# A score product over 128 rows instead of 64, its other half zeros, and narrower bias tiles

## The chip, the core and the metric

The kernel runs on one core of a Trainium2 chip. The metric is the device time of one execution in microseconds, the median of several runs. TensorE multiplies matrices into PSUM; VectorE, ScalarE and GpSimd work element by element, and a queue on SyncE issues the transfers between DRAM and SBUF.

## What is computed

One layer of a hybrid decoder trunk on an input of 2048 tokens by 1024 features: a normalization, one input projection, three parallel branches (differential attention, a gated short convolution, an RWKV-7 recurrence), an output projection, a residual and a last normalization. The change touches attention alone. Each of its 4 heads has two maps of width 64, whose causal softmaxes are subtracted:

```python
qf = (q.astype(jnp.float32) * scale).reshape(b, nb, Q_BLOCK, h, 2, ATT_QK_DIM).swapaxes(0, 1)
...
bias = jnp.transpose(table[t5_causal_bucket(dist)], (2, 0, 1))
logits = jnp.einsum('bqhmd,bkhmd->bhmqk', qb, kf) + bias[None, :, None]
logits = jnp.where(dist >= 0, logits, NEG_INF)
p = jax.nn.softmax(logits, axis=-1)
a = p[:, :, 0] - lam * p[:, :, 1]
return jnp.einsum('bhqk,bkhd->bqhd', a, vf)
```

## The kernel before

All large products are made in a rounded 32-bit format. To keep precision, an operand is split into a high part (the rounded value) and a low part (what is left), and a product is the sum of high by high, high by low and low by high. The work is in two halves of 1024 tokens. In each half an RWKV stage is followed by an attention stage; between their products TensorE gets products of a filler stream (the input projection on line 343, in the second half the output projection on line 1194), a number of them after each step that the stages' code states. TensorE's order is that in which the code is written; the other engines' and the DMA queue's order is set by a scheduler when the program is built.

In `attention`, `load_k` brings 512 columns of K for a head into `rawk`, each map's 64 rows twice, one copy over rows 0 to 63 and one over 64 to 127. GpSimd rounds it into `K` (line 861) and, for each map, replaces the copy in the other map's rows by the low part (line 864). So 128 rows of `K[:, m]` hold high and low part of map m. `load_q` does likewise for 256 queries: `QH` (line 889) holds the high part of a map's queries in both copies, so that one product over 128 rows is high by high plus high by low. `QL` (line 893) holds the low part, 64 rows for each map. `load_v` splits V in the same way.

`scores` goes through the blocks of up to 512 keys of a tile of 128 queries. For each map it makes a pair of products into a score buffer `S` of PSUM (there are three): line 937 with `QH` over 128 rows, line 938 with `QL` over 64 rows, with the queries as the stationary operand and K as the moving one. Then VectorE adds the bias where the block lies near the diagonal (line 942, from the tile `bt` of the head), takes the maximum (line 943), and ScalarE the exponential (line 946), which frees the buffer. `combine` scales and subtracts the two maps (VectorE on line 986); `values` transposes the result (line 1021), splits it (ScalarE on line 1027, VectorE on line 1028) and multiplies with V (lines 1012 to 1014). `att_setup` prepares the bias tiles once, early, by way of DRAM (line 840).

Of the kernel before, what the change touches and what calls it, by code (L numbers as in the profile page):

```python
# [30 lines left out]
GW = 32 // NG  # L31
# [114 lines left out]
def trunk(ctx, tc, a, o, phases="RTO"):  # L146
# [62 lines left out]
    def dtile(name, shape):  # L209
        return dr.tile(list(shape), F32, name=name)  # L210

    # row blocks of the gated mix, transposed: heads by 256 tokens, conv and rwkv by 512
    mixd = [[dtile(f"mx{k}_{i}", (P, 256 if k < 4 else 512)) for i in range(8 if k < 4 else 4)] for k in range(8)]
    pT = {}

# [6 lines left out]
    hh = [[None] * NK, [None] * NK]  # L222
    hl = [[None] * NK, [None] * NK]

    # ------------------------------------------------------------------ normalized input
    def stats(c):
        """1/rms of the tokens of a chunk of the second half, one column per 128 tokens."""
        t0 = HT + c * CK
        ss = cp.tile([P, 2, 4], F32, name=f"ss1{c}")
        for j in range(4):  # L230
            for i in range(2):
                xt = e2("xt")
                dma(xt, a["x"][t0 + j * P:t0 + (j + 1) * P, i * CK:(i + 1) * CK])
                act(xt, xt, AF.Square, accum_out=ss[:, i, j:j + 1])
        tt(ss[:, 0], ss[:, 0], ss[:, 1], ALU.add)
        ts(ss[:, 0], ss[:, 0], 1.0 / D, NORM_EPS, ALU.mult, ALU.add)
        rs = cp.tile([P, 4], F32, name=f"rs1{c}")
        nc.gpsimd.tensor_tensor(rs, ss[:, 0], mexp[:, :4], ALU.pow)
        return rs
# [24 lines left out]
    rscale = [None, None]  # L264

    def stats0(c, xs, pool, raw):
        """1/rms of the tokens, broadcast; with raw, the products with the unscaled input come first."""
        acc = [pool.tile([P, CK], F32, name="acc0", bufs=2) for _ in range(2)]
        for k in range(NK):
            if raw:  # L270
                hh[c][k] = pool.tile([P, CK], F32R, name=f"xh{k}")
                hl[c][k] = pool.tile([P, CK], F32R, name=f"xl{k}")
                act(hh[c][k], xs[k], AF.Copy, scale=V("norm_g", k))
                stt(hl[c][k], xs[k], V("norm_g", k), hh[c][k].bitcast(F32), ALU.mult, ALU.subtract)
            add = nc.gpsimd.tensor_tensor if k % 2 else tt
            if k < 2:
                act(acc[k], xs[k], AF.Square)
            else:
                sq = pool.tile([P, CK], F32, name="sq0", bufs=3)
                act(sq, xs[k], AF.Square)  # L280
                add(acc[k % 2], acc[k % 2], sq, ALU.add)

        def finish():
            sp = pw("ss0")
            for j in range(4):
                for i in range(2):
                    mm(sp[:, j:j + 1], acc[i][:, j * P:(j + 1) * P], C("ones"), start=(i == 0), stop=(i == 1))
            ss = cp.tile([P, 4], F32, name=f"ss0{c}")
            ts(ss, sp[:, 0:4], 1.0 / D, NORM_EPS, ALU.mult, ALU.add)
            rs = cp.tile([P, 4], F32, name=f"rs0{c}")  # L290
            nc.gpsimd.tensor_tensor(rs, ss, mexp[:, :4], ALU.pow)
            return rs

        return finish
# [10 lines left out]
            dma(xk, a["xT"][k * P:(k + 1) * P, t0:t0 + CK])  # L305
            scale_h(c, k, xk, bc, nc.gpsimd.tensor_tensor if k % 2 else tt)

    # ------------------------------------------------------------------ input projection
    wpool = [None]

    early_w = {}
# [92 lines left out]
        yield from inproj(T_RW + i, ev, chunks)  # L404

    def both(*steps):
        """The products of the steps, for the first chunk of all of them before the second."""
        for c in range(2):
            for f, args in steps:
                yield from f(*args, (c,))  # L410
            yield ("chunk", c)
# [39 lines left out]
        return [(inproj, (T_CC + ct, ev_cc)), (inproj, (T_CH + ct, ev_ch)), (inproj, (T_CB + ct, ev_cb)),  # L451
                (inproj, (T_ZC + ct, ev_zc))]

    # ------------------------------------------------------------------ rwkv
    def rwkv(half, pool):
        conr = pool.tile([P, NCONR], F32, name="conr")
        dma(conr, a["conr"])
# [173 lines left out]

        def inverse(s):
            U, Z = s["U"], s["Z"]
            # inverses of the 32x32 diagonal blocks by forward substitution, GW columns of one block per partition;
            # the odd rows are first freed of the even rows before them, so that two rows go at a time
            pr = T("U2", (P, 32, 16))
            Uf = U.rearrange("p s t -> p (s t)")
            tt(pr, U[:, :, 0:32:2], Uf[:, 1:1024:66].unsqueeze(1).broadcast_to([P, 32, 16]), ALU.mult)
# [21 lines left out]
        def late(s):  # L660
# [27 lines left out]
            stt(Z64[:, :, 32:64], p5.rearrange("p (q n) -> p q n", n=32), mB[:, 1:2], Z64[:, :, 32:64], ALU.mult,  # L688
                ALU.add)
            yield LQ[0]  # L690
            # [W | U0]
            W = T("W", (P, NQ, 64))
            wu = pS("wu")
            for h in range(2):
# [9 lines left out]
                nc.gpsimd.memset(Z[r0:r0 + 32, :, r0 + 32:r0 + 64], 0.0)  # L704
            dP4 = dP.rearrange("p (j e) n -> p j e n", e=2)
            yield LQ[1]
            # transition matrices and the read-out of the incoming state
            M = T("M", (P, NJ, 2, 64))
            RW = T("RW", (P, NJ, 2, 64))
            for e in range(2):  # L710
# [23 lines left out]
            for c in range(NC):  # L734
# [8 lines left out]
                    mm(yp[hs, c * 64:(c + 1) * 64], prev[hs], RW[hs, c // 2, c % 2], start=False, stop=True,  # L743
                       skip_group_check=True)
                yield LQ[2]
            # group norm, bonus, gate
            Y = T("Y", bufs=2)
            sq = T("sqy", bufs=2)
            act(sq, yp, AF.Square)
# [24 lines left out]
        st = [dict() for _ in units]  # L774

        def chain(n):
            """The way of a unit up to the inverse; the scores may not start before the unit two back has been read."""
            if n < len(units):
                yield from early(st[n], n, *units[n])
                yield "free"  # L780
                yield from scores(st[n])
                inverse(st[n])
# [28 lines left out]
                    yield x  # L811
            yield WAIT[1]

    # ------------------------------------------------------------------ attention
    def att_setup(pool):
        rel = pool.tile([32, 4], F32, name="rel")
        dma(rel, a["rel"])
# [13 lines left out]
        for h in range(4):  # L831
            bp = pw("bp")
            mm(bp[:, 0:256], rel[:, h:h + 1].broadcast_to([32, P]), oh, start=True, stop=True)
            bz = pool.tile([P, 512], F32, name="bz", bufs=2)
            nc.gpsimd.memset(bz[:, 256:], NEG)
            cpy(bz[:, 0:256], bp[:, 0:256])
            bd = dtile(f"bd{h}", (P * 512,))
            dma(bd.rearrange("(p w) -> p w", p=P), bz)
            b = cp.tile([P, 384], F32, name=f"bt{h}")
            dma(b, bd[127:127 + 128 * 511].rearrange("(p w) -> p w", p=P)[:, 0:384])  # L840
            bt.append(b)
        return nlam, bt

    def attention(half, nlam, bt, pool, after=None):
        """One softmax row tile (128 queries) after the other; the matrix products with V of the pairs of tiles
        that are finished lie between the score blocks of the next ones."""
        pb, kb_, vb_ = PB[half], KB_[half], VB_[half]
        nch = 2 * half + 2
        small = dict(tag="sm", bufs=SM)

        def load_k(h, kc):
            kd = need(f"k{h}", kc)
# [25 lines left out]
        def load_q(h, pr):  # L878
            qc, qo = half * 2 + pr // 2, (pr % 2) * 256
            qd = need(f"q{h}", qc)  # L880
            raw = pool.tile([P, 2, 256], F32, name="rawq", bufs=1)
            for m in range(2):
                for d in range(2):
                    dma(raw[d * 64:d * 64 + 64, m], qd[m * 64:m * 64 + 64, qo:qo + 256])
            QH = pool.tile([P, 2, 256], F32R, name="QH", bufs=2)
            if ON_ACT[3]:
                cpy(QH, raw)
            else:
                nc.gpsimd.tensor_scalar(QH, raw, 1.0, 1.0, ALU.mult, ALU.mult)
            QL = pool.tile([P, 256], F32R, name="QL", bufs=2)  # L890
            for m in range(2):
                ms = slice(m * 64, m * 64 + 64)
                nc.gpsimd.tensor_tensor(QL[ms], raw[ms, m], QH[ms, m].bitcast(F32), ALU.subtract)
            return QH, QL

        class Ahead:
            """Chunks in the order of use, loaded as early as their buffers allow."""

            def __init__(self, load, keys, bufs, there):
                self.load, self.keys, self.bufs, self.have, self.next, self.freed = load, keys, bufs, {}, 0, 0  # L900
# [23 lines left out]
        def scores(t):  # L924
# [6 lines left out]
            for g, (g0, gw) in enumerate(t["groups"]):  # L931
                K = Ks.get((h, g))
                for m in range(2):
                    s = pS("S")
                    ms = slice(m * 64, m * 64 + 64)
                    sw = max(gw, 256)
                    mm(s[:, 0:sw], QH[:, m, off:off + P], K[:, m, 0:sw], start=True, stop=False)  # L937
                    mm(s[:, 0:sw], QL[ms, off:off + P], K[ms, m, 0:sw], start=False, stop=True)  # L938
                    lo, hi = max(b0, g0), g0 + gw
                    if hi > lo:  # L940
                        bo = lo - (i - 1) * P
# [135 lines left out]
        state = dict(wait=0, credit=0.0)  # L1077

        def tick(force=False):
            """One step of the work that is behind; False when there is none."""  # L1080
            did = False
            if tails:
                did = True
# [56 lines left out]
        while tick():  # L1140
            yield UNIT[half]

    # ------------------------------------------------------------------ output
    def out_setup(n):
        """A half of the columns of W_out, in the place of a chunk of the normalized input."""
        W = {"h": [], "l": []}
        for k in range(NK):
            wr = e2("wor")
# [65 lines left out]
                stt(xs[n], xs[n], ss[:, 1:2], gs[n], ALU.mult, ALU.mult)  # L1214
            dma(o["out"][t0:t0 + P, n * CK:(n + 1) * CK], xs[n])

    # ------------------------------------------------------------------ order of the work
    def seq(steps, on_chunk):
        """The steps chunk by chunk, with what is to be done after a chunk."""
        for x in both(*steps):  # L1220
            if isinstance(x, tuple):
                on_chunk(x[1])
            else:
                yield x
# [28 lines left out]
    state = dict(end=False, owed=0.0, used=0.0, allowed=8)  # L1253

    def pull():
        """The next product of the filler stream; False when there is none that may run."""
        if state.get("held") is not None:
            if state["held"] >= state["allowed"]:
                return False
# [119 lines left out]
```

## Time and profile before

| | |
|---|---|
| time, median of 3 runs | 1854.19 us (1853.9 to 1865.09) |
| profiled execution, first to last instruction | 1855.8 us |
| TensorE products, share of the span | 1723.0 us, 93% |
| VectorE | 1228.7 us, 66% |
| ScalarE | 737.5 us, 40% |
| GpSimd | 817.9 us, 44% |
| mean granted clock of TensorE | 0.955 of full speed |

The profile is of one execution, whose span lies 1.6 us above the median. A TensorE product's recorded duration reaches from its start to the modelled end of its drain, so durations of neighbours overlap; the distance from start to start tells what one costs in a stream. PE stands for TensorE's products, PEld for its weight loads, DVE for VectorE, ACT for ScalarE, POOL for GpSimd.

### The profile page before, as it was taken

To read this page: it belongs to the slowest core of one execution; us is meant where nothing else is said; L and a number is where in the kernel's file an instruction comes from. 1 tells how busy PE (TensorE), PEld (TensorE's weight loads), DVE (VectorE), ACT (ScalarE), POOL (GpSimd) and SP (SyncE) were. 2 spreads that over 40 slices of the span, in tenths; PEclk is the share of its full clock that TensorE was granted. 3 is DMA by queue.
4 is the path that set the end of the run, shared out by engine and by line. 5 is a ranking of instruction groups with operands and counts; after the bars stand their busy time and mean duration, and the time that the engine had idled before them with its cause. 6 is when DMAs were issued, how large, how long until landed. Compare 5 with 4: busy or idle time off the path is not lost.

```text
span 1855.8 us, 27286 instructions
## 1 busy us (share of the span) xinstructions
PE 1723.0 (93%) x9416; PEld 1288.3 (69%) x9416; DVE 1228.7 (66%) x2653; ACT 737.5 (40%) x1797; POOL 817.9 (44%) x786
## 2 busy tenths in 40 slices
PE   5899799999999889999799999999999989999998
PEld 4687576777776666777666767766666666767686
DVE  7534866656527888756766576357788888777742
ACT  5331111221126555532122221145565656666642
POOL 6443332333286776334222233473485473453233
PEclk8899898998999999999799998999999989999999
DMA  5342121222156442124222222351142243232223
GB/s 181 114 146 93 47 63 59 86 76 67 61 181 196 148 140 82 64 68 148 63 82 68 86 76 62 100 154 60 63 147 64 74 150 101 71 95 70 81 78 116
DMA packets 136586, 180.13 MB, mean 97 GB/s; under 512 B 34912, under 2 KB 83072, under 8 KB 136448
## 3 DMA queue, kind: packets, MB, share of 16 engines
q1 hardware_dynamic: 136448, 178.39, 30.8%
q8 instruction: 74, 1.21, 0.3%
q14 instruction: 64, 0.52, 0.1%
HBM read 132.18 MB, written 46.14 MB: 96 GB/s over the span
## 4 chain that ended last, share of the span: by engine, by line
PE 62%; DVE 25%; DMA 4%; issue 3%; SPq 2%; ACT 2%; POOL 1%; DVEq 0%; POOLq 0%; ACTq 0%
PE pj L343 27%; PE ops L1194 9%; PE S L938 6%; DVE tmpx L646 5%; PE aT L1021 3%; PE S L937 3%; DVE Xs L649 3%; PE G L572 2%; PE av L1012 2%; DVE P L986 2%; SPq L594 2%; PE av L1014 2%; PE av L1013 2%; DVE x L242 1%; DVE nm L943 1%
## 5 line engine op out<-in xcount | busy, mean ns | idle before, releaser
L343 PE MATMUL pj<-hh,wh 128*128 128x512 f32 x1008 | 424.4, 421 | 4.2 <-DVE raw L394 3.4
L343 PE MATMUL pj<-hl,wh 128*128 128x512 f32 x1008 | 423.8, 420 | 0.0
L343 PE MATMUL pj<-hh,wl 128*128 128x512 f32 x1008 | 423.2, 420 | 0.0
L946 ACT ACTIVATE P<-S,nm 128x512 f32<-128x512 f32 (+3 forms) x320 | 199.3, 623 | 162.9 <-DVE nm L943 143.6
L943 DVE TENSOR_REDUCE nm<-S 128x1 f32<-128x512 f32 (+3 forms) x320 | 192.5, 606 | 77.4 <-PE S L938 74.1
L329 POOL TENSOR_TENSOR wl<-wr,wh 128x1024 fp32r<-128x1024 f32 x85 | 209.6, 2465 | 46.8 <-ACT wh L324 41.2
L343 PEld LDWEIGHTS pj<-hh,wh 128*128 128x128 f32 x1008 | 195.9, 194 | 49.1 <-issue 7.6
L343 PEld LDWEIGHTS pj<-hl,wh 128*128 128x128 f32 x1008 | 195.7, 194 | 45.2 <-issue 9.7
L343 PEld LDWEIGHTS pj<-hh,wl 128*128 128x128 f32 x1008 | 195.4, 194 | 45.0 <-issue 7.9
L938 PE MATMUL S<-K,QL 64*128 64x512 f32 (+2 forms) x320 | 150.1, 469 | 0.0
L326 POOL TENSOR_SCALAR wh<-wr 128x1024 fp32r<-128x1024 f32 x70 | 76.5, 1093 | 162.5 <-PE pj L343 152.6
L986 DVE SCALAR_TENSOR_TENSOR P<-P,sc 128x512 f32<-128x512 f32 (+3 forms) x160 | 141.5, 910 | 4.5 <-ACT P L970 2.9
L646 DVE TENSOR_TENSOR tmpx<-U,Xs 128x16 f32<-128x16 f32 (+15 forms) x256 | 128.6, 502 | 6.6 <-POOL U L640 1.2
L938 PEld LDWEIGHTS S<-K,QL 64*128 64x128 f32 x320 | 58.8, 184 | 101.6 <-issue 99.4
L937 PE MATMUL S<-K,QH 128*128 128x512 f32 (+2 forms) x320 | 120.8, 378 | 8.0 <-ACT P L946 8.0
L1028 DVE TENSOR_TENSOR aTl<-aT,aTh 128x512 fp32r<-128x512 f32 x144 | 98.4, 686 | 35.2 <-ACT aTh L1027 34.4
L1027 ACT CAST aTh<-aT 128x512 fp32r<-128x512 f32 x144 | 83.7, 585 | 87.9 <-PE aT L1021 87.1
L942 DVE TENSOR_TENSOR S<-S,bt 128x256 f32<-128x256 f32 (+1 forms) x152 | 57.4, 379 | 90.6 <-PE S L938 86.6
L1021 PE MATMUL aT<-con,P 128*128 128x128 f32 x576 | 93.9, 289 | 22.4 <-DVE aTl L1028 17.4
L1194 PE MATMUL ops<-woh,wl 128*128 128x512 f32 x256 | 103.9, 406 | 0.0
L1194 PE MATMUL ops<-woh,wh 128*128 128x512 f32 x256 | 103.5, 404 | 0.0
L1194 PE MATMUL ops<-wol,wh 128*128 128x512 f32 x256 | 103.5, 404 | 0.0
(336 smaller groups left out, 3354.2 us busy)
## 6 DMA issues: line engine op xcount, KB each, us to landing
wr<-in_wt_dram SPq DMA_DIRECT2D x85, 512.0 KB, 3.7
rawk<-pk SPq DMA_DIRECT2D x96, 128.0 KB, 2.8
U<-ud SPq DMA_DIRECT2D x128, 64.0 KB, 2.2
rawq<-pq SPq DMA_DIRECT2D x128, 64.0 KB, 2.3
wr<-mx SPq DMA_DIRECT2D x128, 64.0 KB, 1.9
oxt<-in_x_dram SPq DMA_DIRECT2D x32, 256.0 KB, 3.2
out_dram<-oxt SPq DMA_DIRECT2D x32, 256.0 KB, 2.1
prw<-s SPq DMA_DIRECT2D x28, 256.0 KB, 2.1
```

The costliest lines, as they stand in the source:

```text
L329: nc.gpsimd.tensor_tensor(wl[:, ks], wr[:, ks], wh[:, ks].bitcast(F32), ALU.subtract)
L343: mm(ps, lhs[:, k], rhs[c][k], start=(n == 0), stop=(n == 3 * NK - 1))
L646: tt(tmp[:, :, :, 0:m], U[:, 0:m, i:i + 2].rearrange("p j r -> p r j").unsqueeze(2).broadcast_to([P, 2, GW, m]), Xs[:, 0:m].rearrange("p j ...
L937: mm(s[:, 0:sw], QH[:, m, off:off + P], K[:, m, 0:sw], start=True, stop=False)
L938: mm(s[:, 0:sw], QL[ms, off:off + P], K[ms, m, 0:sw], start=False, stop=True)
L943: nc.vector.tensor_reduce(nm[:, m, g:g + 1], s[:, 0:gw], AX.X, ALU.max, negate=True)
L946: act(p[:, 0:gw], s[:, 0:gw], AF.Exp, bias=nm[:, m, g:g + 1], accum_out=l[:, m, g:g + 1])
L986: stt(p1, p1, sc[:, 1, g:g + 1], p0, ALU.mult, ALU.add)
L1021: nc.tensor.transpose(t[:, d * 256 + qi * P:d * 256 + qi * P + P], x["A"][g][:, ko:ko + P], ident)
L1027: cpy(th, t)
L1028: tt(tl, t, th.bitcast(F32), ALU.subtract)
L1194: mm(ps, l[:, k], Ws[n][r][k], start=(c == 0), stop=(c == 3 * NK - 1))
```

## The change

The low part of the queries gets one 128-row tile of two maps. For each map its own 64 rows hold the low part, and the other 64 rows zeros, which are written once at the start of an attention stage; two such tiles are used in turn. The product on line 938 (944 after the change) then contracts over all 128 rows; the zero rows meet K's low part and add nothing. The bias tiles keep 256 of their 384 columns. Some comment lines are also gone, which moves no instruction.

```diff
-            b = cp.tile([P, 384], F32, name=f"bt{h}")
-            dma(b, bd[127:127 + 128 * 511].rearrange("(p w) -> p w", p=P)[:, 0:384])
+            b = cp.tile([P, 256], F32, name=f"bt{h}")
+            dma(b, bd[127:127 + 128 * 511].rearrange("(p w) -> p w", p=P)[:, 0:256])
...
+        lows = [pool.tile([P, 2, 256], F32R, name=f"QL{i}") for i in range(2)]
+        for x in lows:
+            for m in range(2):
+                os = slice(64 - m * 64, 128 - m * 64)
+                nc.gpsimd.memset(x[os, m].bitcast(F32), 0.0)
...
-            QL = pool.tile([P, 256], F32R, name="QL", bufs=2)
+            QL = lows[(h * 4 + pr) % 2]
             for m in range(2):
                 ms = slice(m * 64, m * 64 + 64)
-                nc.gpsimd.tensor_tensor(QL[ms], raw[ms, m], QH[ms, m].bitcast(F32), ALU.subtract)
+                nc.gpsimd.tensor_tensor(QL[ms, m], raw[ms, m], QH[ms, m].bitcast(F32), ALU.subtract)
...
                     s = pS("S")
-                    ms = slice(m * 64, m * 64 + 64)
                     sw = max(gw, 256)
                     mm(s[:, 0:sw], QH[:, m, off:off + P], K[:, m, 0:sw], start=True, stop=False)
-                    mm(s[:, 0:sw], QL[ms, off:off + P], K[ms, m, 0:sw], start=False, stop=True)
+                    mm(s[:, 0:sw], QL[:, m, off:off + P], K[:, m, 0:sw], start=False, stop=True)
```

On TensorE, at a score pair of the first attention stage, where the filler's products (`pj`) stand ahead of the pair and the transposes of probabilities (`aT`) behind it, the order before is this:

```order
L343 MATMUL pj_0_5693<-hh_6_616,wl 128x512
L343 MATMUL pj_0_5693<-hh_7_621,wh 128x512
L937 MATMUL S<-K,QH 128x512
L938 MATMUL S<-K,QL 128x512
L1021 MATMUL aT<-con,P 128x128 x4
```

The same place after the change, where the lines have moved by 6:

```order
L343 MATMUL pj_0_5691<-hh_6_616,wl 128x512
L343 MATMUL pj_0_5691<-hh_7_621,wh 128x512
L943 MATMUL S<-K,QH 128x512
L944 MATMUL S<-K,QL_4602 128x512
L1027 MATMUL aT<-con,P 128x128 x4
```

Nothing has moved here; the second product of the pair reads the tile with the zeros. On GpSimd, at the start of the first attention stage (`wh` and `wl` are the filler's weights, `K`, `QH`, `QL` and `V` the first chunks of the stage), the order before is this:

```order
L326 TENSOR_SCALAR wh<-wr 128x1024
L329 TENSOR_TENSOR wl<-wr,wh 128x1024
L861 TENSOR_SCALAR K<-rawk 128x1024
L864 TENSOR_TENSOR K<-rawk,K 64x512 x2
L889 TENSOR_SCALAR QH<-rawq 128x512
L874 TENSOR_SCALAR V<-vr 128x512
L893 TENSOR_TENSOR QL<-rawq,QH 64x256 x2
```

The same place after the change:

```order
L326 TENSOR_SCALAR wh<-wr 128x1024
L856 MEMSET QL_4602 64x256 x2
L856 MEMSET QL_4603 64x256 x2
L329 TENSOR_TENSOR wl<-wr,wh 128x1024
L868 TENSOR_SCALAR K<-rawk 128x1024
L871 TENSOR_TENSOR K<-rawk,K 64x512 x2
L896 TENSOR_SCALAR QH<-rawq 128x512
L881 TENSOR_SCALAR V<-vr 128x512
L900 TENSOR_TENSOR QL_4602<-rawq,QH 64x256 x2
```

Four clears now stand ahead of the split of the filler's weights and of the stage's first conversions; in the second stage they stand at the corresponding place, behind that split.

## Rows read from the trace of the kernel before

**Rows 1.** The page: span, and busy time of each engine with its share.

```profile
span 1855.8 us, 27286 instructions
PE 1723.0 (93%) x9416; PEld 1288.3 (69%) x9416; DVE 1228.7 (66%) x2653; ACT 737.5 (40%) x1797; POOL 817.9 (44%) x786
```

**Rows 2.** Stretches: length, PE, PEld, DVE, ACT, POOL busy (count), clock, DMA.

```profile
541.50:790.50 249.00, 232.61 (x1078) 164.92 (x1078) 193.43 (x427) 142.72 (x386) 159.19 (x163) 0.97 0.41 128
1219.60:1765.50 545.90, 525.98 (x2444) 366.96 (x2443) 436.43 (x822) 333.52 (x813) 268.37 (x238) 0.98 0.30 91
616.50:691.50 75.00, 66.89 (x321) 47.91 (x321) 62.06 (x129) 39.04 (x100) 58.86 (x55) 0.95 0.44 135
691.50:716.50 25.00, 20.86 (x102) 15.86 (x101) 22.64 (x37) 15.58 (x39) 18.29 (x16) 0.93 0.37 120
1344.60:1394.60 50.00, 45.66 (x211) 32.24 (x210) 44.48 (x79) 29.54 (x71) 41.67 (x35) 0.95 0.46 142
1494.60:1519.60 25.00, 18.28 (x79) 13.84 (x80) 22.33 (x33) 13.40 (x34) 17.92 (x13) 0.80 0.45 139
```

**Rows 3.** VectorE's waits in the two attention stages: us in total, times, longest.

```profile
DVE S L942 <- PE S L938: 57.0, 40, 26.8
DVE nm L943 <- PE S L938: 11.4, 15, 1.3
...
DVE nm L943 <- PE S L938: 62.7, 47, 26.8
DVE S L942 <- PE S L938: 29.0, 37, 2.4
```

**Rows 4.** TensorE's waits in the second attention stage, same columns.

```profile
PE aT L1021 <- DVE aTl L1028: 7.4, 6, 4.4
```

**Rows 5.** TensorE's groups by form: busy us, mean ns of one.

```profile
L938 PE MATMUL S<-K,QL 64*128 64x512 f32 x224 | 111.3, 497 | 0.0
...
L937 PE MATMUL S<-K,QH 128*128 128x512 f32 x224 | 91.3, 407 | 7.3 <-ACT P L946 7.3
```

**Rows 6.** TensorE's timeline from 1301.9 us: start, duration, product.

```profile
1301.92 0.40 PE L937 MATMUL S<-K,QH 128*128 128x512 f32 x1
1302.25 0.49 PE L938 MATMUL S<-K,QL 64*128 64x512 f32 x1
1302.67 0.50 PE L343 MATMUL pj<-hh,wl 128*128 128x512 f32 x1
1303.01 0.40 PE L343 MATMUL pj<-hh,wh 128*128 128x512 f32 x1
...
1303.47 0.39 PE L343 MATMUL pj<-hh,wl 128*128 128x512 f32 x1
1303.70 0.39 PE L937 MATMUL S<-K,QH 128*128 128x512 f32 x1
```

**Rows 7.** Weight loads from 1303.4 us, with the load engine's idle time ahead of each.

```profile
1303.47 0.19 PEld L937 LDWEIGHTS S<-K,QH 128*128 128x128 f32 x1
1304.02 0.18 PEld L938 LDWEIGHTS S<-K,QL 64*128 64x128 f32 x1 [0.35 <-issue]
1304.45 0.19 PEld L343 LDWEIGHTS pj<-hh,wh 128*128 128x128 f32 x1 [0.25 <-issue]
```

**Rows 8.** Line 938 alone in the two attention stages: busy us and count on PE, PEld.

```profile
541.50:790.50 249.00, 43.22 (x96) 17.64 (x96) 0.97 0.41 128
1219.60:1765.50 545.90, 106.90 (x224) 41.13 (x224) 0.98 0.30 91
```

**Rows 9.** GpSimd's clears in the first attention stage.

```profile
L988 POOL MEMSET P<- 128x128 f32 x16 | 3.2, 203 | 2.2 <-DVE P L986 1.8 <-PE aT L1021 0.2
```

**Rows 10.** GpSimd's timeline before the first attention stage.

```profile
522.03 1.55 POOL L893 TENSOR_TENSOR QL<-rawq,QH 64x256 fp32r<-64x256 f32 x2
```

**Rows 11.** GpSimd's waits for K in the second attention stage.

```profile
POOL K L861 <- PE S L938: 13.1, 4, 9.9
POOL K L861 <- DMA rawk<-pk: 13.1, 5, 5.7
```

## The prediction

> **What bounds the kernel now.** I began with the page's busy shares: TensorE 93% over the span, VectorE 66% [rows 1]. An average doesn't say what a change in two stages is worth, so the second view is the table by stretches for the two stages in which scores are made, 541.5 to 790.5 us and 1219.6 to 1765.5 us [rows 2]. TensorE is busy 232.6 of 249.0 us in the first and 526.0 of 545.9 us in the second, at a granted clock of 0.97 and 0.98. VectorE is busy 193.4 and 436.4 us, ScalarE and GpSimd less. So TensorE sets the pace, and VectorE, which takes every score block out of PSUM (bias, maximum), stands some 20% behind it. The third view is who waited for whom there: VectorE's largest waits are those for the product on line 938 [rows 3], while TensorE's largest named wait is 7.4 us [rows 4]. Work taken from TensorE in these stages shortens them until VectorE is full.
>
> **What a score block costs TensorE.** Mean durations by form show something odd: the product with the low part (line 938), which contracts over 64 rows, takes 497 ns for 512 columns, and the one with the high part (line 937), over 128 rows and the same columns, 407 ns [rows 5]. Durations overlap, so I price by starts in the timeline [rows 6]. In a stream of 128-row products of 512 columns one starts every 0.23 us (1303.47, 1303.70, and two steps from 1303.01 to 1303.47). Around a pair that breaks: from line 937 to line 938 0.33 us, from line 938 to the next product 0.42, and from that to the one behind it 0.34 (1301.92, 1302.25, 1302.67, 1303.01); then 0.23 again. The excess is 0.10 + 0.19 + 0.11 = 0.40 us a pair. The weight loads tell why [rows 7]. Those of 128-row products start about one product ahead of their own (1303.47 for the product at 1303.70), but that of line 938 starts with its product, at 1304.02, 0.35 us after the load engine fell idle, and that of the product behind it at 1304.45, also with its own. Each change between the 64-row and the 128-row form waits until the array has run empty and then loads in the open, twice for each pair.
>
> TensorE: Matmul & The Clock Gate, a page of the Trainium skill, states in its summary table at the end ("Why this matters for your kernels") that a single product over 32 rows takes the same time as one over 128. By that rule the 64-row product is no dearer than the full one and the sum would be nothing; the rows differ, because they price the switch and not the streaming.
>
> **The change part by part.**
> 1. *The 320 products of line 938 over 128 rows.* The column count and the order on TensorE stay the same: the pair still stands between the same neighbours (first two order listings). After the change line 938 has the form of line 937, so its neighbours have no change of form beside them. Saved per pair: 0.40 us where a 512-column product follows, and I expect less where a transpose or a product with V does; the sure part is 0.10 + 0.19 = 0.29 us (the third step is the successor's own). Blocks of 256 or 384 columns pay for the same two changes of form, so they count in full. I take 0.37 for the mix. 96 pairs in the first stage, 224 in the second [rows 8]: 0.37 x 96 = 36 us and 0.37 x 224 = 83 us, 118 us of TensorE's time in all; ends 0.29 x 320 = 93 and 0.40 x 320 = 128.
> 2. *What VectorE lets through.* Nothing of its work changes. With the 118 us gone TensorE would need 249.0 - 36 = 213 and 545.9 - 83 = 463 us, against 193.4 and 436.4 us of VectorE: it would have to be busy 91% and 94% of the stages. How full can it get? I looked for stretches in which it already is ahead of TensorE, so that its chain sets the pace: 691.5 to 716.5 us, 22.64 of 25.0 (91%); 1344.6 to 1394.6, 44.48 of 50.0 (89%); 1494.6 to 1519.6, 22.33 of 25.0 (89%); weaker, 616.5 to 691.5, 62.06 of 75.0 (83%) [rows 2]. I take 89%: the stages then last 193.4 / 0.89 = 217 and 436.4 / 0.89 = 490 us, a gain of 32 and 56 us, **88 us**. At 85% it is 228 and 513, a gain of 21 and 32, 53 us. A second way to see it: VectorE can't gain more than it waits for scores now. That is 57.0 + 11.4 us in the first stage and 62.7 + 29.0 in the second, of which 26.8 each is one wait that began ahead of the stage: 42 and 65 us. So the first stage may give all of its 36, the second at most 65 of 83, 101 together. 88 lies between the two.
> 3. *Zeros, on GpSimd.* Each stage clears four quarters of the two tiles (64x256). The nearest row, a 128x128 clear, has a mean of 203 ns [rows 9]; twice the columns give 0.2 to 0.4 us each, 1 to 2 us a stage. They stand ahead of the first K, Q and V conversions in GpSimd's queue (last two listings); the split of the filler's weights stands behind them too in the first stage. In the trace the first Q low part is made at 522.03 to 523.58 us [rows 10] and the first score product is at 541.5, so 18 us of cover hide this. Cost 0; 2 to 4 us for both stages if that cover were gone.
> 4. *The low part itself* is subtracted by as many instructions of the same 64x256 shape, into another place of the tile; two tiles in turn as before. Cost 0. A few rows of GpSimd's and the DMA queue's order change places with their neighbours in the first stage; GpSimd is busy 159 of 249 us there [rows 2], so I put that at 0, with 3 us either way in the range.
> 5. *Narrower bias tiles.* A tile of 128 queries at row block i takes the bias of keys from block i - 1 on, at most 256 columns, so line 942 reads what it read; only the four set-up DMAs get shorter, issued once ahead of the first RWKV stage. Cost 0.
>
> **Sum:** 1855.8 us (the profiled span) - 88 = 1768. The timed median is 1854.19, 1.6 below this span, so the forecast is **1766 us**, 4.8% less. What comes next as the limit is VectorE in both stages, with TensorE waiting at the transposes of line 1021 and for free score buffers at line 937.
>
> **The rivals.**
> - *TensorE's whole saving arrives* (VectorE fills its gaps to 94%). For it: the three score buffers let TensorE run ahead of a late VectorE, and over the whole second stage no named wait of TensorE is above 7.4 us now [rows 4]. Against: the stretches above. Gain 106 to 128, centre 118: 1736 us. Chance 0.12.
> - *The supply of K takes the place.* GpSimd waits for raw K from DRAM, 13.1 us over five waits in the second stage, the longest 5.7 [rows 11]; there is one raw buffer, and a faster TensorE asks sooner. 24 chunks of K are loaded in the two stages (8 and 16); at the mean of those waits, 13.1 / 5 = 2.6 us, 24 of them in the way are 63 us and leave 88 - 63 = 25: 1829 us. Against: GpSimd also waits 13.1 us for TensorE to free K, so it is mostly ahead. Chance 0.07.
> - *The form isn't the cause.* Each 64-row product is also the last of its PSUM block, and closing a block could cost the same steps. Against: the filler's products close a block of PSUM after every 24 and keep their step of 0.23 us, and the open weight load [rows 7] stands ahead of the 64-row product, not only behind it. Then nothing is gained: 1854 us. Chance 0.04.
> - *Slower: full-row weight loads stay in the open.* If a 128-row load could not run beside a 128-row product, a pair in its new form would show three loads (both of its own and the successor's) of 0.19 us, 0.57 us, against 0.37 saved: 320 x 0.20 = 64 us more, 1918 us. It decides from two open loads a pair on. Against: the load at 1303.47 runs beside the product of 1303.47, both over 128 rows [rows 6, 7]. Chance 0.03. TensorE: Matmul & The Clock Gate of the Trainium skill, "Part 3", "The mechanism", speaks for this rival: loads overlap running products only when the row group differs. By that rule the change would take away an overlap; the trace disagrees, as the 0.19 us load at 1303.47 shows.
>
> **How the numbers follow.** The forecast (a gain of 55 to 105 us) has the remaining 0.74. The range reaches from the whole saving, 1855.8 - 120 - 1.6 = 1734, to 1808, a gain of 46 us, between VectorE at 85% and the supply's case; it leaves out that case and the two without a gain (0.14), and the outer end of the first rival. A measurement of this kernel can tell about 1% from no change, 18 us. Faster: 0.74 + 0.12 + 0.06 of the supply's 0.07 = 0.92; within 1%: 0.04 + 0.01 = 0.05; slower: 0.03.
>
> **What the changed profile would show.** Steps 1: line 938's successor (line 944 there) at the 407 ns of the 128-row form, starts 0.23 us apart through a pair, the weight load of the low part one product ahead, and the idle time of the load engine ahead of it gone. Step 2: stages of about 217 and 490 us, VectorE at 87 to 91% in both, TensorE's waits for line 1028 grown from 7.4 us to tens of us, those for line 946 likewise, and perhaps more stretches at the lower granted clock, as at 1494.6 to 1519.6 us (0.80) where it waits now. Steps 3 to 5: clears of 0.2 to 0.4 us and no later first score product; the rest of the program unchanged. I would be wrong if the steps stay at 0.33 and 0.42 us, or if VectorE holds below 85%.

## The result and the profile after

The changed kernel takes 1793.78 us (median of 4 runs, 1790.98 to 1798.8) against 1854.05 us before on the same chip: ratio 0.967, 95% interval 0.9639 to 0.97. That is 60 us less, where 88 had been forecast; the time lies in the range. The profiled execution has a span of 1789.2 us.

The page of the changed kernel answers to [rows 1]: TensorE has 107 us less of recorded products, VectorE the same work.

```profile
span 1789.2 us, 27288 instructions
PE 1615.6 (90%) x9416; PEld 1300.2 (73%) x9416; DVE 1229.6 (69%) x2653; ACT 733.4 (41%) x1797; POOL 822.4 (46%) x794
```

The low-part product (now line 944) by form, mean in ns, answers to [rows 5]:

```profile
L943 PE MATMUL S<-K,QH 128*128 128x512 f32 x224 | 93.8, 419 | 20.3 <-ACT P L952 20.0
L944 PE MATMUL S<-K,QL 128*128 128x512 f32 x224 | 89.3, 399 | 0.0
```

TensorE's timeline at a pair, starts and durations in us, answers to [rows 6]:

```profile
1302.17 0.39 PE L343 MATMUL pj<-hh,wl 128*128 128x512 f32 x1
1302.40 0.39 PE L943 MATMUL S<-K,QH 128*128 128x512 f32 x1
1302.63 0.40 PE L944 MATMUL S<-K,QL 128*128 128x512 f32 x1
1302.86 0.28 PE L1018 MATMUL av<-aTh,V 128*128 128x256 f32 x1
1302.98 0.27 PE L1019 MATMUL av<-aTh,V 128*128 128x256 f32 x1
```

The weight loads of the same stretch answer to [rows 7]:

```profile
1302.17 0.19 PEld L943 LDWEIGHTS S<-K,QH 128*128 128x128 f32 x1
1302.40 0.19 PEld L944 LDWEIGHTS S<-K,QL 128*128 128x128 f32 x1
1302.63 0.19 PEld L1018 LDWEIGHTS av<-aTh,V 128*128 128x128 f32 x1
```

Through the pair a product now starts every 0.23 us, and the load of the low part (1302.40) runs one product ahead of its own (1302.63). The step of 0.42 us is gone, and so is the load in the open.

The two attention stages, from their first score product to their last, answer to [rows 2]:

```profile
542.80:775.70 232.90, 204.94 (x1077) 170.86 (x1076) 192.90 (x426) 140.66 (x383) 159.94 (x163) 0.95 0.43 136
1198.90:1698.40 499.50, 452.26 (x2443) 378.20 (x2442) 434.49 (x821) 329.24 (x809) 269.56 (x238) 0.97 0.32 100
```

The columns are length, PE, PEld, DVE, ACT, POOL busy, granted clock, DMA share and GB/s. Measured between the same products, the stages lasted 248.3 and 545.4 us before, so they gained 15.4 and 45.9 us, 61 in all; the other 5 us between the two spans lie outside. VectorE is busy 83% and 87% of the stages after the change.

TensorE's waits in the first and the second stage (us in total, times, longest) answer to [rows 4]:

```profile
PE av L1020 <- DVE aTl L1034: 6.9, 5, 4.0
PE aT L1027 <- DVE aTl L1034: 6.0, 5, 2.3
PE pj L343 <- DVE th L361: 3.8, 2, 3.2
PE aT L1027 <- DVE P L992: 3.6, 5, 1.9
PE S L943 <- ACT P L952: 3.4, 4, 2.5
...
PE S L943 <- ACT P L952: 18.4, 12, 4.3
PE aT L1027 <- DVE aTl L1034: 16.2, 12, 5.3
PE obc L1066 <- POOL orp L1061: 6.9, 3, 3.8
PE aT L1027 <- DVE P L992: 3.5, 2, 3.2
```

To see where TensorE's time went I added up, over both stages, the step from each product's start to the next one's, and took off the step that the same neighbours have at full clock without a wait (the shortest third of their steps after the change). What is left falls into four sorts:

| us over both stages | before | after |
|---|---|---|
| sum of the regular steps | 596.7 | 596.7 |
| steps at a score pair | 120.5 | 8.2 |
| steps ahead of a product that waited | 43.3 | 87.0 |
| steps at the lower granted clock | 15.6 | 22.3 |
| other | 17.6 | 18.3 |
| both stages | 793.7 | 732.4 |

So 112 us were freed, close to the forecast's 118. Of these 44 went into waits, 7 into more time at the lower of TensorE's two clocks, and 61 arrived.

A wait, seen on four engines. On VectorE, two of the combining steps of line 992 (`P<-P,sc`), which take 0.74 us each when left alone, last 4.36 us together, the first of them 3.75:

```profile
1213.49 1.43 DVE L992 SCALAR_TENSOR_TENSOR P<-P,sc 128x512 f32<-128x512 f32 x1
1214.84 0.42 DVE L948 TENSOR_TENSOR S<-S,bt 128x256 f32<-128x256 f32 x1
1215.18 4.36 DVE L992 SCALAR_TENSOR_TENSOR P<-P,sc 128x512 f32<-128x512 f32 x2
1219.46 0.41 DVE L949 TENSOR_REDUCE nm<-S 128x1 f32<-128x256 f32 x1
```

GpSimd meanwhile works without a gap, on two-operand subtractions for V and for the filler's weights and then on a one-operand step:

```profile
1214.30 1.78 POOL L882 TENSOR_TENSOR V<-vr,V 128x512 fp32r<-128x512 f32 x1
1216.03 2.34 POOL L329 TENSOR_TENSOR wl<-wr,wh 128x1024 fp32r<-128x1024 f32 x1
1218.34 1.06 POOL L896 TENSOR_SCALAR QH<-rawq 128x512 fp32r<-128x512 f32 x1
```

ScalarE has stood idle for 5.52 us before its exponential, and TensorE for 4.13 us before the product that needs the freed score buffer:

```profile
1219.91 0.47 ACT L952 ACTIVATE P<-S,nm 128x256 f32<-128x256 f32 x1 [5.52 <-DVE nm L949]
```

```profile
1216.00 0.40 PE L343 MATMUL pj<-hh,wl 128*128 128x512 f32 x1
1220.53 0.79 PE L943 MATMUL S<-K,QH 128*128 128x512 f32 x1 [4.13 <-ACT P L952]
```

### The profile page after: what moved, and what is told of

Read it like the earlier page. It is cut to its first block, busy times and chain, and to the rows that moved or that the text cites. A ratio compares the mean times of both kernels' runs of the same rounds, so it can differ in the third digit from the quotient of the medians.

```text
span 1789.2 us, 27288 instructions
## 1 busy us (share of the span) xinstructions
PE 1615.6 (90%) x9416; PEld 1300.2 (73%) x9416; DVE 1229.6 (69%) x2653; ACT 733.4 (41%) x1797; POOL 822.4 (46%) x794
## 4 chain that ended last, share of the span: by engine, by line
PE 48%; DVE 33%; DMA 5%; issue 4%; ACT 4%; SPq 3%; POOL 3%; DVEq 0%; POOLq 0%; ACTq 0%
PE pj L343 23%; PE ops L1200 7%; DVE tmpx L646 5%; DVE P L992 4%; DVE Xs L649 3%; PE aT L1027 3%; DVE nm L949 3%; PE G L572 2%; SPq L594 2%; PE S L943 2%; PE S L944 2%; PE av L1020 2%; PE av L1018 1%; PE av L1019 1%; DVE x L242 1%
## 5 line engine op out<-in xcount | busy, mean ns | idle before, releaser
L992 DVE SCALAR_TENSOR_TENSOR P<-P,sc 128x512 f32<-128x512 f32 (+3 forms) x160 | 148.0, 950 | 6.8 <-ACT P L976 4.6
L943 PE MATMUL S<-K,QH 128*128 128x512 f32 (+2 forms) x320 | 124.8, 390 | 22.2 <-ACT P L952 21.9
L944 PE MATMUL S<-K,QL 128*128 128x512 f32 (+2 forms) x320 | 119.0, 372 | 0.0
L1027 PEld LDWEIGHTS aT<-con,P 128*128 128x128 f32 x576 | 70.0, 144 | 58.2 <-DVE aTl L1034 29.9
```

What stands on the lines that cost most here:

```text
L944: mm(s[:, 0:sw], QL[:, m, off:off + P], K[:, m, 0:sw], start=False, stop=True)
L992: stt(p1, p1, sc[:, 1, g:g + 1], p0, ALU.mult, ALU.add)
L1027: nc.tensor.transpose(t[:, d * 256 + qi * P:d * 256 + qi * P + P], x["A"][g][:, ko:ko + P], ident)
```

## The experiments

The kernels of one group ran on one chip together with the kernel before. The distance is that between a variant of the changed kernel and the same variant of the kernel before; without a variant it is 60 us by medians and 61 in the attention stages.

**The narrow bias tiles alone.**

```diff
-            b = cp.tile([P, 384], F32, name=f"bt{h}")
+            b = cp.tile([P, 256], F32, name=f"bt{h}")
```

> The kernel before with bias tiles of 256 columns, the products unchanged. My theory (all of the gain comes from the change of form on TensorE): the time of before, 1854 us, within 6 us. Rival (the smaller footprint or the shorter transfers carry part of it): 1835 us or less.

1858.42 us, ratio 0.9973 to 1.0033 of the kernel before: within some 6 us, no part of the gain comes from the bias tiles.

**All but the 128 rows.** The clears, the tiles of two maps and the bias tiles of the changed kernel, with the second product over 64 rows:

```diff
-                    mm(s[:, 0:sw], QL[:, m, off:off + P], K[:, m, 0:sw], start=False, stop=True)
+                    mm(s[:, 0:sw], QL[ms, m, off:off + P], K[ms, m, 0:sw], start=False, stop=True)
```

> The changed kernel with its clears, its low tiles of two maps and its narrow bias tiles, but with the second product over 64 rows again. My theory: 1854 us within 8, the steps around a pair back at 0.33 and 0.42 us. Rival (clears and the moved rows on GpSimd cost the part that did not arrive, 28 us against the forecast): 1870 to 1885 us.

1860.59 us, ratio 0.9976 to 1.0031. TensorE's timeline of this kernel (the pair is lines 944 and 945):

```profile
1304.87 0.40 PE L944 MATMUL S<-K,QH 128*128 128x512 f32 x1
1305.19 0.49 PE L945 MATMUL S<-K,QL 64*128 64x512 f32 x1
1305.62 0.50 PE L343 MATMUL pj<-hh,wl 128*128 128x512 f32 x1
1305.95 0.40 PE L343 MATMUL pj<-hh,wh 128*128 128x512 f32 x1
```

The steps of 0.32, 0.43 and 0.33 us are back. Clears and moved rows cost nothing that can be measured, and in the changed kernel the eight clears take 0.31 us each, the last at 1175.8 us, well ahead of the second stage's first score product at 1198.6. They did not hold back the missing part; the row count of the second product is the whole of the gain.

**Less work on VectorE.** The maximum over half of a block, in the kernel before and in the changed one:

```diff
-                    nc.vector.tensor_reduce(nm[:, m, g:g + 1], s[:, 0:gw], AX.X, ALU.max, negate=True)
+                    nc.vector.tensor_reduce(nm[:, m, g:g + 1], s[:, 0:gw // 2], AX.X, ALU.max, negate=True)
```

> The kernel before; the maximum of a score block is taken over half of its columns, so that VectorE has some 0.25 us less for each of the 320 blocks (80 us in all; the result is not the softmax of the reference). My theory: TensorE sets the pace here, so little comes of it, 10 to 30 us from its waits for VectorE: 1825 to 1845 us. Rival (supply of K and Q or the clock): no matter, 1845 to 1855 us.

> The changed kernel with the maximum over half of the columns. My theory (the part of the 118 us that did not arrive is held by VectorE's chain): the distance to the same kernel before grows from 60 to 85 us or more, 1735 to 1760 us. Rival (supply of K by GpSimd and DMA, or the extra half clock, holds it): the distance stays at 55 to 70 us, 1765 to 1785 us.

1855.46 us (ratio 0.9968 to 1.0018) and 1773.53 us (0.9503 to 0.9595 of the kernel before). The first expectation missed: nothing came of it. The second missed too: the time lies in the rival's range, and the medians' distance of 82 us between the two bounds. The distance of the two profiled spans is 74 us, that of the attention stages only 66; the profiled execution of the changed kernel with half the maximum took 1781.66 us, the longest of its four, so where the rest of the medians' distance lies it doesn't show. The stages of the changed kernel with half the maximum:

```profile
541.90:772.80 230.90, 206.51 (x1077) 171.07 (x1076) 179.26 (x426) 138.65 (x382) 160.72 (x163) 0.94 0.45 138
1193.90:1689.60 495.70, 454.84 (x2442) 382.13 (x2441) 391.35 (x821) 325.89 (x809) 267.06 (x239) 0.96 0.32 101
```

VectorE has 13.6 + 43.1 = 57 us less to do, and the stages are 2.0 + 3.8 us shorter. Sorted as in the table above, TensorE's waits fall from 87 to some 76 us, and the steps at the lower clock grow from 22 to 28. VectorE is now busy 78% and 79%, and TensorE still waits. That VectorE is simply full, which is how the forecast had put it, falls here. What was left to look at was when single VectorE instructions are late.

**A shorter step on GpSimd.** The low parts of the weights and of the mixed rows are filled by a copy with one operand, so the result is not that of the reference. The copy also takes less than half the time, 1.05 us in place of 2.40 for the weights, and no run separates the two. The edit:

```diff
-            nc.gpsimd.tensor_tensor(wl[:, ks], wr[:, ks], wh[:, ks].bitcast(F32), ALU.subtract)
+            nc.gpsimd.tensor_scalar(wl[:, ks], wr[:, ks], 1.0, 1.0, ALU.mult, ALU.mult)
...
-        nc.gpsimd.tensor_tensor(ml, mr, mh.bitcast(F32), ALU.subtract)
+        nc.gpsimd.tensor_scalar(ml, mr, 1.0, 1.0, ALU.mult, ALU.mult)
```

> The kernel before; GpSimd fills the low part of the weights and of the mixed rows by a copy with one operand instead of a subtraction with two (2.4 us each, 101 of them), so the low parts are not those of the reference. New theory (the missing part of the 118 us goes into waits of TensorE behind VectorE instructions that are held up for 2 to 5 us beside two-operand work of GpSimd): TensorE is late by itself here, so 1825 to 1850 us in all, and the attention stages get 5 to 12 us shorter. Rival (VectorE is simply full, whatever GpSimd does): 1850 to 1858 us.

> The changed kernel with the same copy in place of the subtraction. New theory: the lengthening of VectorE's instructions in the second stage falls from 89 us to under 60, TensorE's waits in both stages together from 87 to under 60 us, and the distance to the same kernel before grows from 62 to 80 us or more: 1745 to 1770 us. Rival (VectorE full, or the chain of the score buffers by itself): the distance stays at 62 us, 1785 to 1795 us.

In these expectations and the next ones, 87 us are the steps ahead of waiting products in the table above, and the lengthening is the sum, over VectorE's instructions of the second stage, of what each takes above the shortest of its line and shape (the fifth percentile). 1798.99 us (0.9689 to 0.973) and 1714.15 us (0.9233 to 0.9273). Both came out below every range that had been given, since the kernel before gained some 50 us outside of the attention stages, which the theory had not counted. The distance is 84.8 us, on the theory's side. The attention stages of the two kernels, before and changed:

```profile
518.00:766.80 248.80, 233.74 (x1076) 165.48 (x1075) 188.45 (x426) 141.65 (x384) 137.18 (x161) 0.97 0.40 127
1167.90:1706.30 538.40, 524.21 (x2443) 365.32 (x2442) 407.70 (x822) 331.49 (x812) 225.90 (x236) 0.98 0.30 92
```

```profile
514.10:741.70 227.60, 202.31 (x1075) 169.26 (x1075) 184.84 (x425) 140.27 (x383) 138.68 (x161) 0.96 0.44 138
1143.80:1623.30 479.50, 445.94 (x2442) 375.93 (x2441) 404.67 (x822) 330.73 (x812) 226.56 (x237) 0.98 0.34 103
```

The change is worth 787.2 - 707.1 = 80 us here, 19 more than with the subtraction. The mean of the combining step in the second stage, with the subtraction and then with the copy:

```profile
L992 DVE SCALAR_TENSOR_TENSOR P<-P,sc 128x512 f32<-128x512 f32 x84 | 86.0, 1053 | 4.3 <-ACT P L976 3.8
```

```profile
L992 DVE SCALAR_TENSOR_TENSOR P<-P,sc 128x512 f32<-128x512 f32 x84 | 72.1, 889 | 1.7 <-ACT P L976 1.4
```

The maximum, which reads PSUM, in the same stage with the subtraction:

```profile
L949 DVE TENSOR_REDUCE nm<-S 128x1 f32<-128x512 f32 x174 | 117.2, 683 | 42.6 <-PE S L944 41.4
```

In the whole changed kernel the 224 maxima over 512 columns take 0.67 to 0.69 us each, the 112 combining steps over 512 columns 0.74 to 3.75. VectorE's lengthening in the second stage falls from 89 to 58 us with the copy, and its instructions of over 1.5 us in both stages from 46 to 20. TensorE's waits fall from 87 to 68, not to the 60 that were expected. In the kernel before, the copy takes them from 43 to some 35, so the change now adds 32 us of waits in place of 44, and no time at the lower clock in place of 7: of the 19 us some 11 are waits and 8 the clock.

**GpSimd's subtractions in pieces.** The result stays exact:

```diff
-WSP = 1
+WSP = 8
...
-        nc.gpsimd.tensor_tensor(ml, mr, mh.bitcast(F32), ALU.subtract)
+        for k in range(NK):
+            nc.gpsimd.tensor_tensor(ml[:, k], mr[:, k], mh[:, k].bitcast(F32), ALU.subtract)
```

> The changed kernel, exact result, with GpSimd's subtractions for the low part of the weights and of the mixed rows cut into 8 pieces of 128 columns. New theory, if VectorE gets in between two pieces: the longest VectorE instructions in the attention stages fall from 3.7 us to under 1.5 and the time to 1770 to 1785 us. If it does not get in between, or each piece costs a start of its own, 1790 to 1805 us.

> The kernel before, exact result, with GpSimd's subtractions for the low part of the weights and of the mixed rows in 8 pieces. Theory (VectorE held up beside GpSimd costs TensorE its waits, in the RWKV stages too): 1820 to 1835 us, a distance of 65 to 85 us to the changed kernel in pieces (1752.9). Rival (the pieces help only where the change has made TensorE faster): 1845 to 1858 us.

1752.85 us (0.9447 to 0.9483 of the kernel before), 41 us under the changed kernel and better than forecast, and 1816.48 us (0.9762 to 0.986) without the change. VectorE's instructions of over 1.5 us in the attention stages fall from 46 to 18, but not all under 1.5 us as expected: the longest takes 4.28 us. The kernel before and the distance came out a little below their expected ranges. The distance is 64 us, and 58 in the attention stages, so the pieces give as much with the change as without. The waits are some 32 us before the change and 75 after it: the change adds 43 us of them, as it does without the pieces, although as many long VectorE instructions are gone as with the copy. Most of the 41 us lies outside the attention stages, which became 2 and 9 us shorter; outside of them VectorE's instructions of over 1.5 us fall from 54 to 10. This is the fastest kernel of the study with an exact result.

> The changed kernel in pieces, with the subtractions for the low parts of K and V in pieces of 128 columns as well; exact result. Theory: a little more of the same, 1742 to 1752 us, most of it in the second attention stage. Rival (the starts of more instructions on GpSimd outweigh it, and K comes later): 1752 to 1765 us.

1768.63 us (0.9524 to 0.9583): 16 us slower than with the first pieces alone, more than even the rival said. TensorE's waits of this kernel in the second stage:

```profile
PE obc L1070 <- POOL orp L1065: 20.6, 6, 7.8
PE S L947 <- ACT P L956: 18.7, 9, 9.0
```

The second stage is 11 us longer than with the first pieces alone, and GpSimd is busy 329 us of it against 306. For the small power step on line 1065 (line 1061 without these pieces) TensorE waited 6.9 us in the changed kernel and already 15.2 with the first pieces; now it is 20.6. The wait for score buffers grows from 13.9 to 18.7 us, and nearly half of it is one wait, behind a VectorE instruction on six columns:

```profile
1321.29 9.52 DVE L971 TENSOR_TENSOR l<-l,e 128x6 f32<-128x6 f32 x1 [0.23 <-ACT e L969]
```

```profile
1318.32 4.32 POOL L873 TENSOR_TENSOR K<-rawk,K 64x128 fp32r<-64x128 f32 x8
...
1330.75 1.26 POOL L1163 TENSOR_TENSOR wol<-wor,woh 128x512 fp32r<-128x512 f32 x1
```

```profile
1334.03 0.69 PE L947 MATMUL S<-K,QH 128*128 128x384 f32 x1 [9.01 <-ACT P L956]
```

While that instruction lasts, GpSimd goes from one instruction to the next without a gap. So VectorE can be held up through a whole row of GpSimd instructions, pieces among them, and not for the length of one alone.

**The place of the filler.** `SCALE` sets how much of the filler goes with each step of the four stages:

```diff
-SCALE = (0.6, 1.0, 0.55, 1.0)
+SCALE = (0.55, 1.15, 0.5, 1.15)
```

> The changed kernel with 15% more of the filler's products for each step of the attention stages and 8% fewer in the RWKV stages. If TensorE now stands idle in the attention stages and not elsewhere, the work placed there is hidden: 1770 to 1788 us. Rival (the stages get longer by what is added, and the RWKV stages are held by VectorE's chain anyway): 1790 to 1810 us.

1832.88 us (0.9854 to 0.9936): the rival's side, and past it. Its two attention stages:

```profile
537.60:791.20 253.60, 221.58 (x1151) 186.16 (x1150) 200.04 (x427) 143.61 (x389) 159.96 (x164) 0.93 0.41 130
1215.20:1743.70 528.50, 470.19 (x2489) 393.45 (x2488) 435.22 (x825) 332.45 (x815) 270.26 (x241) 0.95 0.31 95
```

They are 21 and 29 us longer than in the changed kernel, though the products added are worth 16 and 11 us by their regular steps. TensorE's idle time there is no room for more work.

> The changed kernel in pieces with 10% fewer of the filler's products for each step of the attention stages and some 8% more in the RWKV stages; exact result. More filler there cost 39 us. If the optimum lies on the other side of the setting: 1735 to 1750 us; if the setting is near it (TensorE then waits longer for VectorE in the attention stages): 1755 to 1780 us.

That was the kernel in pieces with `SCALE = (0.65, 0.9, 0.6, 0.9)`: 1797.63 us (0.9658 to 0.9735), 45 us slower than with the old numbers and outside both bounds. The attention stages took 724.5 us against 721.8 with the old numbers, though they hold some 140 products fewer: fewer products on TensorE do not shorten them there. Neither direction helped, though the two were tried on different kernels.

**Both reliefs together.** The changed kernel with the copy on GpSimd, scaled this time, and half the maximum.

> The changed kernel with both reliefs: the maximum over half of the columns, and GpSimd's copy (scaled to 0.00001 of the value) in place of its two-operand subtraction; the result is not that of the reference. If the waits of TensorE that are left (68 us with the copy alone) come from VectorE's load: they fall to 45 us or less, 1690 to 1700 us. If they come from the chain through ScalarE and VectorE in a fixed order: 55 us or more, 1705 to 1715 us.

1711.33 us (0.9208 to 0.9265), 3 us under the copy alone, which the two intervals do not tell apart. The waits are 63 us. TensorE's largest named ones in the second stage:

```profile
PE S L943 <- ACT P L952: 12.6, 11, 3.7
PE obc L1066 <- POOL orp L1061: 10.9, 5, 4.4
PE aT L1027 <- DVE aTl L1034: 7.7, 8, 2.0
```

With VectorE busy 78% and 77% these stay nearly as they were with the copy alone (13.3, 7.5 and 8.7 us), the second side of the expectation.

## Why the prediction was right, and where its size was off

- *Step 1, the price of a pair:* right. 0.40 us was read from the starts, 118 us were forecast and 112 were freed. The kernel with everything but the 128 rows shows that it is the row count and nothing else. TensorEngine Tiling (Array Packing), a page of the Trainium skill, says in "Key Properties" that a change of the tiling mode drains TensorE. The trace is in line with it and prices the two changes round one product at 0.40 us; the drain itself it doesn't show. The rule on single products that the prediction set against its sum does not tell the cost of standing among full ones.
- *Step 2, what VectorE lets through:* the mis-sized term. I took 89% as the share to which VectorE can be filled; it measured 83% in the first stage (232.9 us against 217 forecast) and 87% in the second (499.5 against 490). Below 85% was one of the prediction's own signs of being wrong, so the first stage failed it. The stretches from which I took 89% were short and were those in which VectorE's work happened to be dense; over a stage TensorE and VectorE take turns in waiting: from 542.7 to 620 us TensorE is busy 93% and VectorE 78%, from 620 to 720 us 79% and 85%. The row at 83% over 75 us [rows 2], which I called weaker, was the better one for the first stage. The word "full" was wrong as well: 57 us less work on VectorE shortened the stages by 6. And VectorE's busy time was not all work: measured like the 89 us above, 87 of its 436 us in the second stage were lengthening before the change already. That the time still fell into the range is owed to the range's width, not to this step.
- *What held the missing part:* 51 us of the 112 went into waits (44) and lower clock (7). The copy on GpSimd raised the gain in the stages by 19 us, 11 of it waits, and cut the long VectorE instructions by more than half, and the wait of 4.13 us shown above stands behind one of them. So part of the waits stands behind VectorE instructions held up beside GpSimd's work. How large a part is not shown: the pieces removed as many long instructions and left the growth of the waits as it was (43 us), and before the change there were 41 long ones against 46 after it, so their number does not decide it. SBUF — State Buffer, a page of the Trainium skill, states in "Who interferes with whom" that a VectorE instruction with two operands in SBUF contends with a GpSimd instruction that reads SBUF. The trace agrees: the combining steps of line 992, with both operands in SBUF, take 0.74 to 3.75 us, while no maximum on line 949, which reads PSUM, takes over 0.69.
- *What stays open:* with both reliefs TensorE still waits 63 us. In most of these waits VectorE is at work on line 992, 1034 or 949, so its order in the queue and its chain with ScalarE and the three score buffers remain the likely cause. That was argued from the traces; no run here changed the number of score buffers, or VectorE's order by itself.
- *Steps 3 to 5:* right. Clears (0.31 us each), moved rows and bias tiles are worth nothing measurable.
- *The rivals:* that the closing of a block was the cause falls, since the second product still closes its block and the long steps are gone. The supply of K was not it, since no wait of TensorE for K stands among its larger ones in the changed kernel. Open loads of full rows don't occur. More time at the lower clock came as forecast (0.97 to 0.95 and 0.98 to 0.97 in the stages) and cost 7 us.

## What to carry to other kernels

Price a product by the starts around it, not by its duration: a product over fewer rows can cost its neighbours more than its own streaming, and padding it with zeros to the neighbours' form then pays. When the bounding engine is relieved, less can arrive than the next engine's busy share leaves room for: here 61 of 112 us, with that engine at 83 and 87%. Read the share from long stretches, and look for the instructions of that engine that last several times their usual time, though to remove them did not by itself bring the rest. GpSimd's steps hold up VectorE instructions that work on SBUF alone, such as those of line 992, and not those that read PSUM; eight shorter ones in the place of one took 41 us off here, most of it outside the stages of the change. Cutting further steps as well lost 16 us again: GpSimd came later, and a row of its work without a gap held one VectorE instruction for 9.52 us.

## What was not expected of the hardware

- A VectorE instruction on three columns (line 974 before the change) took 3.51 us at 1235.6 us, beside GpSimd's subtractions; in the stages 41 VectorE instructions took over 1.5 us before the change and 46 after it.
- Cutting GpSimd's subtraction of 128x1024 into eight took 37 us off the kernel before (1853 to 1816), 13.5 of it in the attention stages (793.7 to 780.2) and the rest outside of them, which had not been in view at all.
- Halving the columns of 320 VectorE maxima changed the time of the kernel before by nothing that could be measured (0.9968 to 1.0018).
